# Turning gated activation tiles by a transposing DMA on 16-bit halves instead of on TensorE

## The chip, the cores and the metric

The kernel runs on one core of one Trainium2 chip. TensorE multiplies (its operands come from SBUF, its results go to banks in PSUM), VectorE and ScalarE work element by element, SP issues DMAs, and each engine runs its own list of instructions in order, waiting on semaphores. The metric is the device time of one execution in microseconds; lower is better.

## The reference

One layer on a sequence of 256 tokens of width 2048, in 32-bit floating point: a half-step SwiGLU feed-forward block (FFN 1), a token-mixing layer (a recurrent branch and a gated convolution behind one input projection and ahead of one output projection), and a second feed-forward block (FFN 2). The change lies in the feed-forward blocks, whose inner width is 5632:

```
def swiglu_ffn(x, w_gate, w_up, w_down):
    return (jax.nn.silu(x @ w_gate) * (x @ w_up)) @ w_down
...
x = x + FFN_RESIDUAL_SCALE * swiglu_ffn(rms_norm(x, ffn1_norm[l]),
                                        ffn1_w_gate[l], ffn1_w_up[l], ffn1_w_down[l])
```

## The kernel before

**Products.** Every 32-bit product is made of three products in `F32R`. A weight unit is 512 rows by 512 columns (128 partitions x 4 x 512, 1 MB); SP loads it into `raw`, ScalarE casts it in two halves of 128x1024 into `hi`, VectorE subtracts to get `lo` (128x2048). The stationary operand, the activations, has a high and a low of its own, and `multiply` runs high x hi, low x hi and high x lo: 12 matmuls of 128x512 for one half of the tokens (t = 0 or 1), 24 for both. Buffers for `raw` (three, and two longer kept ones) and for `hi`/`lo` (two, and one more) limit how far ahead the other engines can work.

**Groups.** The inner width is 11 units of 512. Unit 0 comes first, alone (`begin` in FFN 1, `begin_after` in FFN 2). The others come in five pairs, s = 0 to 4, units 1 + 2s and 2 + 2s. For each pair `seven` makes the gate group and then the up group, each with seven products in place of eight for half of the contraction (a Strassen-like scheme with sums of blocks, `raw <- raw - raw` on VectorE) and plain products for the rest. `gate` and `up` are called as results are done: `up` multiplies into the tile `sg[t, n]` (128 tokens x 512 columns; in the profile these tiles are named `u_g`, `z` and `s_g`, and `sg` for unit 0), first for n = 1, then for n = 0.

**Turning.** For the product with the down weights a tile must have its columns on the partitions. `turn_hidden(u, t, h, again)` makes four TensorE transposes of 128x128 into the PSUM bank `ph`, ScalarE casts the result to the high part of `hidden[u]`, VectorE subtracts for the low part, and where `again` is set (even s) ScalarE copies the turned tile back, for the sums of blocks. The calls are put into `waiting` and made by `settle` a little later, so that TensorE has other matmuls meanwhile.

**Down.** After s = 0, 2 and 4 `down` multiplies the units that are ready: after s = 0 units 0, 1, 2; after s = 2 units 3 to 6; after s = 4 units 7 to 10. The output has four columns of 512: column 0 by `product`, then sums of blocks of the last two units m and n, then columns 1 and 2 by `seven`, then column 3 by `product`. In `product` the order of units is the older ones, n, m.

**Order.** The kernel is written in a framework that schedules: it puts the instructions of each engine in an order of its own, by its estimates, except where the kernel pins program order. So the order on an engine is not that of the code.

Of the kernel before, what the change touches and what calls it, by code (L numbers as in the profile page):

```python
# [9 lines left out]

F32 = mybir.dt.float32
F32R = mybir.dt.float32r
AF = mybir.ActivationFunctionType
ALU = mybir.AluOpType
AX = mybir.AxisListType

P = 128
# [3 lines left out]
NT = S // P  # L21
KD = D // P
KF = FF // P
CW = 512
NC_D = D // CW
UK = 4
# [22 lines left out]
def hybrid_block(ctx: ExitStack, tc: tile.TileContext, a: dict, out: bass.AP):  # L49
# [32 lines left out]
    def bank(name):  # L82
        return psum.tile([P, 512], F32, tag="ps", name=name)
# [128 lines left out]
    class Norm:  # L212
# [5 lines left out]
        def squares(self, c, engines=(act, act)):  # L218
            for t, engine in enumerate(engines):
                x, part = xres[:, t, c * CW : (c + 1) * CW], self.ss[:, t, c : c + 1]  # L220
                if engine is dve:
                    junk = work.tile([P, CW], F32, tag="junkv", name=f"junkv_{self.name}_{c}_{t}", bufs=1)
                    dve.scalar_tensor_tensor(junk, x, 1.0, x, op0=ALU.mult, op1=ALU.mult, accum_out=part)
# [69 lines left out]

    def product(w, c, us, y, name, stagger=False, between=None):
        ps = [bank(f"ps_{name}_{t}") for t in range(NT)]
        cs = slice(c * CW, (c + 1) * CW)
        late = []
        for i, u in enumerate(us):  # L300
            blk = unit(w[u * UK * P : (u + 1) * UK * P, cs], f"{name}_{u}")
            begin, end = i == 0, i == len(us) - 1
            if stagger and i >= len(us) - 2:
                late.append((u, blk, begin, end))
            else:
                multiply([(ps[t], stationary(y(u), t), begin, end) for t in range(NT)], blk)
            if between:
                between(i)
            pump(1.5)
        for t in range(NT):  # L310
            for u, blk, begin, end in late:
                multiply([(ps[t], stationary(y(u), t), begin, end)], blk)
        return ps

# [101 lines left out]
    def ffn(tag, norm, after, opening=False):  # L416
        with (
# [7 lines left out]
            def keep(name, dt=F32):  # L425
                return fp.tile([P, CW], dt, tag="keep", name=name, bufs=13)

            hidden = {}
            turned = {}
            waiting = []  # L430
# [17 lines left out]
            def settle():  # L448
                while waiting:
                    turn_hidden(*waiting.pop(0))  # L450


            units, vs, sf, ready = [], {}, {}, []

# [41 lines left out]
            def begin():  # L496
# [26 lines left out]
                for j in range(UK):  # L523
                    for t in range(NT):
# [1 line left out]
                        pe.matmul(gps[t], yh, blk[j][0], start=j == 0, stop=False)  # L526
                        pe.matmul(gps[t], yl, blk[j][0], start=False, stop=False)
                        pe.matmul(gps[t], yh, blk[j][1], start=False, stop=j == UK - 1)
                norm.squares(0, (dve, dve))
                for c in (1, 2):  # L530
                    norm.squares(c, (dve, act))

                def tokens(u):
                    n = [keep(f"n{tag}_{u}_{t}") for t in range(NT)]
# [36 lines left out]
                norm.squares(3, (dve, act))  # L571
# [49 lines left out]
                for t in range(NT):  # L621
                    sg = keep(f"sg{tag}_0_{t}")
                    act.activation(sg, gps[t], AF.Silu)
                    dve.tensor_tensor(sg, ups[t], sg, op=ALU.mult)
                    waiting.append((0, t, sg, False))

            def begin_after():
                follow = {
                    (0, "g"): [flush],
                    (0, "u"): [norm.factor, lambda: plain(0)],  # L630
                    (1, "g"): [norm.rows, lambda: plain(1), lambda: normalise(0)],
                    (1, "u"): [lambda: normalise(1), sums, lambda: plain(2)],
                    (2, "g"): [lambda: normalise(2), lambda: plain(3)],
                }
                for u in range(KD // UK):
                    for m in "gu":
                        blk = parts_of(first_columns(m, u), f"{m}{tag}_0_{u}")
                        multiply([(ps[m, t], stationary(norm.xT[u], t), u == 0, u == 3) for t in range(NT)], blk)
                        pump(1.5)
                        for fn in follow.get((u, m), ()):  # L640
                            fn()
                units.append(big(f"x{tag}_3"))
                for t in range(NT):
                    sg = keep(f"sg{tag}_0_{t}")
                    act.activation(sg, ps["g", t], AF.Silu, scale=norm.r[:, t : t + 1])
                    dve.scalar_tensor_tensor(
                        sg, ps["u", t], norm.r[:, t : t + 1], sg, op0=ALU.mult, op1=ALU.mult
                    )
                    waiting.append((0, t, sg, False))

            (begin if opening else begin_after)()
            xs = list(enumerate(units))[2:]
            turn_of["hold"] = False

            def down(last):
                us = sorted(set(hidden) | {w[0] for w in waiting})
                m, n = us[-2:]
# [8 lines left out]
                for c in (0, 3):  # L666
                    end = last and tag == 2 and c == NC_D - 1
                    ps = product(
                        wd, c, us[:-2] + [n, m], hidden.get, f"d{tag}_{m}_{c}", end,
                        (lambda i: settle()) if c == 0 else None,  # L670
                    )
                    Engine.pinned = end
                    for t in range(NT):
                        update(c, t, ps[t])
                    if c == 0:
                        sh = {}
                        seven_of(
                            sh, hidden[m], hidden[n],
                            {(t, i): turned[u, t] for t in range(NT) for i, u in ((0, m), (1, n))},
                            quad(keep(f"hspare{tag}_{m}")),  # L680
                            [[quad(keep(f"hs{tag}_{m}_{i}_{z}", F32R)) for z in range(2)] for i in range(4)],
                        )()
                        got = {}

                        def add(t, b, ps, tiles):
                            got[t, b] = [ps] + tiles
                            if (0, b) in got and (1, b) in got:
                                for i in range(NT):
                                    update(2 - b, i, *got[i, b])

                        if tag == 1 and m == 5:
                            prepare()
                        seven(wd, (m, n), (2 * CW, CW), sh, [(u, hidden[u]) for u in us[:-2]], f"d{tag}_{m}", keep, add)
                hidden.clear()
                turned.clear()

            for s in range(5):
# [15 lines left out]

                def up(t, n, ps, tiles):
                    dve.tensor_tensor(sg[t, n], total(ps, tiles), sg[t, n], op=ALU.mult)
                    if (t, n) == (1, 0):
                        settle()
                    waiting.append((1 + 2 * s + n, t, sg[t, n], s % 2 == 0))

                def meanwhile(i):  # L720
                    if i == 1:
                        settle()
                    elif s == 0 and not opening:
# [347 lines left out]
```

## Time and profile before

| | |
|---|---|
| median of 3 runs | 1739.5 us (1739.38 to 1740.49) |
| profiled execution, its own time | 1741.48 us |
| span of the profiled execution | 1739.7 us |
| TensorE clock granted | 0.999 |
| busy: TensorE, VectorE, ScalarE | 1721.9, 1485.2, 1042.1 us |
| DMA, mean share of 16 engines on SP's queue | 57.2% |
| `ph`: busy on TensorE, ScalarE, VectorE | 22.97, 37.06, 28.16 us |

Busy is the time in which an engine has an instruction running; on TensorE one matmul overlaps the next, so sums of durations are more than the time that passes. In the rows, `out<-in` are the program's names with buffer numbers left out, `x` is a count, and a bracket or a last column names the idle time ahead of an instruction and what ended it.

### The profile page before, as it was taken

The numbers are of one execution on the slowest core, as the hardware profiler recorded it, in microseconds if no ns is written. First come the engines' busy times: TensorE is split into PE (matmuls) and PEld (weight loads), VectorE is DVE, ScalarE is ACT, GpSimd is POOL, SyncE is SP. The second block draws the span as 40 slices with busy tenths as digits, with TensorE's granted clock in tenths as the row PEclk, the third lists the DMA queues.
The fourth block names the chain that finished last, engine by engine and source line by source line (L and its number), as shares of the span: only waits on it lengthen the run. The fifth ranks groups of instructions, "written<-read, shape, count | busy, mean of one in ns | idle before, by whom it ended". The sixth has DMA issues, their size and how long they took to land. (4 is left out here: it accounts for less than half of the span.)

```text
span 1739.7 us, 20328 instructions
## 1 busy us (share of the span) xinstructions
PE 1721.9 (99%) x8035; PEld 1436.1 (83%) x8035; DVE 1485.2 (85%) x1233; ACT 1042.1 (60%) x1345; POOL 6.9 (0%) x32
## 2 busy tenths in 40 slices
PE   8999999999999999999999999999999999999997
PEld 6888888888888888888888888888788888888886
DVE  7998999889789898687986668989799888899895
ACT  6765566656466656565655555656556664656654
POOL 1000000000000000000000000000000000000000
PEclk9999999999999999999999999999999999999999
DMA  8564665575466656555556663575475546555742
GB/s 299 191 213 145 218 214 197 182 254 205 159 209 203 199 188 216 172 170 194 177 189 209 224 203 129 199 243 185 160 252 201 206 144 231 193 194 194 255 174 104
DMA packets 173920, 343.24 MB, mean 197 GB/s; under 512 B 5636, under 2 KB 8064, under 8 KB 173696
## 3 DMA queue, kind: packets, MB, share of 16 engines
q1 hardware_dynamic: 173360, 340.82, 57.2%
q8 instruction: 63, 1.03, 0.2%
q10 hardware_dynamic: 144, 1.05, 0.1%
q14 instruction: 33, 0.27, 0.0%
q0 software_dynamic: 320, 0.07, 0.0%
HBM read 339.82 MB, written 2.10 MB: 197 GB/s over the span
## 5 line engine op out<-in xcount | busy, mean ns | idle before, releaser
L42 ACT CAST hi_g_p<-raw_g 128x1024 fp32r<-128x1024 f32 x132 | 134.3, 1049 | 97.8 <-DVE raw_g L42 27.6
L42 ACT CAST hi_u_p<-raw_u 128x1024 fp32r<-128x1024 f32 x140 | 140.8, 1047 | 73.1 <-DVE raw_u L42 26.8
L42 DVE TENSOR_TENSOR lo_g_p<-raw_g,hi_g_p 128x2048 fp32r<-128x2048 f32 x66 | 150.2, 2285 | 30.2 <-ACT hi_g_p L42 29.9
L42 DVE TENSOR_TENSOR lo_u_p<-raw_u,hi_u_p 128x2048 fp32r<-128x2048 f32 x70 | 159.0, 2286 | 19.3 <-ACT hi_u_p L42 18.9
L42 PE MATMUL ps_d<-hi_d,h 128*128 128x512 f32 x704 | 168.0, 390 | 0.0
L42 PEld LDWEIGHTS ps_d<-hi_d,h 128*128 128x128 f32 x704 | 131.5, 188 | 27.0
L42 PE MATMUL ps_in<-xT_nm,hi_in 128*128 128x512 f32 x640 | 153.3, 391 | 0.0
L42 PEld LDWEIGHTS ps_in<-xT_nm,hi_in 128*128 128x128 f32 x640 | 117.4, 188 | 23.3 <-ACT tha L42 0.3
L42 ACT CAST hi_d<-raw_d 128x1024 fp32r<-128x1024 f32 x88 | 88.2, 1047 | 68.2 <-PE ps_u_d L42 22.4
L42 DVE TENSOR_TENSOR lo_d<-raw_d,hi_d 128x2048 fp32r<-128x2048 f32 x44 | 100.6, 2290 | 31.0 <-ACT hi_d L42 31.0
L42 DVE TENSOR_TENSOR lo_in<-raw_in,hi_in 128x2048 fp32r<-128x2048 f32 x40 | 91.3, 2286 | 38.8 <-ACT hi_in L42 38.2
L42 ACT CAST hi_in<-raw_in 128x1024 fp32r<-128x1024 f32 x80 | 80.0, 1045 | 67.1 <-PE ps_in L42 45.8
L42 ACT CAST hi_d_p<-raw_d 128x1024 fp32r<-128x1024 f32 x84 | 84.3, 1047 | 50.2 <-DVE raw_d L42 39.4
L42 ACT CAST hi_g_x<-raw_g 128x1024 fp32r<-128x1024 f32 x80 | 81.3, 1048 | 47.5 <-PE ps_g_c L42 25.3
L42 DVE TENSOR_TENSOR lo_d_p<-raw_d,hi_d_p 128x2048 fp32r<-128x2048 f32 x42 | 95.4, 2286 | 11.8 <-ACT hi_d_p L42 11.7
L42 ACT CAST hi_u_x<-raw_u 128x1024 fp32r<-128x1024 f32 x80 | 80.5, 1047 | 33.9 <-PE ps_u_c L42 21.8
L42 DVE TENSOR_TENSOR raw_u<-raw_u,raw_u 128x2048 f32<-128x2048 f32 x40 | 91.6, 2290 | 9.0 <-DMA raw_u<-in_ffn_w_up_dram 8.3
L42 DVE TENSOR_TENSOR lo_g_x<-raw_g,hi_g_x 128x2048 fp32r<-128x2048 f32 x40 | 91.3, 2284 | 5.5 <-ACT hi_g_x L42 5.3
L42 DVE TENSOR_TENSOR raw_g<-raw_g,raw_g 128x2048 f32<-128x2048 f32 x37 | 84.5, 2286 | 9.3 <-DMA raw_g<-in_ffn_w_gate_dram 8.9
L42 DVE TENSOR_TENSOR lo_u_x<-raw_u,hi_u_x 128x2048 fp32r<-128x2048 f32 x40 | 91.4, 2284 | 0.8 <-ACT hi_u_x L42 0.5
L42 PE MATMUL ps_d<-lo_d,h 128*128 128x512 f32 x352 | 87.3, 389 | 0.0
L42 PEld LDWEIGHTS ps_in<-xT_nm,lo_in 128*128 128x128 f32 x640 | 82.1, 191 | 3.1
(391 smaller groups left out, 3592.2 us busy)
## 6 DMA issues: line engine op xcount, KB each, us to landing
raw_d<-in_ffn_w_down_dram SPq DMA_DIRECT2D x88, 1024.0 KB, 5.1
raw_u<-in_ffn_w_up_dram SPq DMA_DIRECT2D x87, 1024.0 KB, 5.2
raw_g<-in_ffn_w_gate_dram SPq DMA_DIRECT2D x86, 1024.0 KB, 5.2
raw_in<-in_w_in_dram SPq DMA_DIRECT2D x40, 1024.0 KB, 5.0
raw_o<-in_w_out_dram SPq DMA_DIRECT2D x16, 1024.0 KB, 5.1
xres<-in_x_dram SPq DMA_DIRECT2D x4, 512.0 KB, 7.6
raw_u<-in_ffn_w_up_dram SPq DMA_DIRECT2D x2, 512.0 KB, 9.3
raw_g_first<-in_ffn_w_gate_dram SPq DMA_DIRECT2D x1, 1024.0 KB, 11.9
```

The costliest lines, as they stand in the source:

```text
L42: ins = getattr(self.engine, name)(*args, **kwargs)
```

## The change

`turn_hidden` is now called at once instead of through `waiting`. ScalarE copies the tile, read as 16-bit numbers, into `plane` with all first halves ahead of all second halves; one DMA on SP's queue transposes the eight 128x128 blocks of 16-bit numbers from `plane` back into the tile; ScalarE copies it into `plane` again so that the halves join to 32-bit numbers; from there the high, the low and the second copy are made as before. There is one buffer for `plane`. The squares that VectorE makes use it as scratch too, instead of one of their own. `down` holds the banks of columns 0 and 3 at the same time and goes through them by a plan: the older units and n for column 0, the older units for column 3 (with one older unit also n), then m for column 0, the sums of blocks, and the rest of column 3 ahead of `seven`, or behind it in the last one.

```
-                pt = bank(f"ph{tag}_{u}_{t}")
-                for j in range(UK):
-                    pe.transpose(pt[:, j * P : (j + 1) * P], h[:, j * P : (j + 1) * P], ident)
+                pt = plane()
+                mixed = "p (f b) -> p b f"
+                flat = "p (b f) -> p b f"
+                act.copy(pt.bitcast(U16).rearrange(flat, b=2), h.bitcast(U16).rearrange(mixed, b=2))
+                nc.sync.dma_start(
+                    h.bitcast(U16).rearrange("p (r c) -> p r c", c=P), pt.bitcast(U16), transpose=True
+                )
+                act.copy(pt.bitcast(U16).rearrange(mixed, b=2), h.bitcast(U16).rearrange(flat, b=2))
                 pt = pt.rearrange("p (j c) -> p j c", j=UK)
...
-                norm.squares(0, (dve, dve))
+                norm.squares(0, (dve, dve), plane)
...
-                    waiting.append((0, t, sg, False))
+                    turn_hidden(0, t, sg, False)
...
+                def add_units(c, units):
+                    blks = [
+                        (u, unit(wd[u * UK * P : (u + 1) * UK * P, c * CW : (c + 1) * CW], f"d{tag}_{m}_{c}_{u}"))
+                        for u in units
+                    ]
...
+                plan = [(0, [u]) for u in others + [n]] + [(3, [u]) for u in others]
+                if len(others) == 1:
+                    plan.append((3, [n]))
+                plan.append((0, [m]))
+                tail = [(3, [n, m])] if end else [(3, [u]) for u in (n, m) if (3, [u]) not in plan]
+                for step in plan:
+                    add_units(*step)
+                block_sums()
+                if not last:
+                    for step in tail:
+                        add_units(*step)
...
+                seven(wd, (m, n), (2 * CW, CW), sh, [(u, hidden[u]) for u in others], f"d{tag}_{m}", keep, add)
+                if last:
+                    for step in tail:
+                        add_units(*step)
...
-                    if (t, n) == (1, 0):
-                        settle()
-                    waiting.append((1 + 2 * s + n, t, sg[t, n], s % 2 == 0))
+                    turn_hidden(1 + 2 * s + n, t, sg[t, n], s % 2 == 0)
```

Three places in the order, all in FFN 1; the places in FFN 2 read alike.

TensorE, end of the up group of s = 2 and start of its down (m = 5, n = 6), before:

```order
L42 MATMUL ph_6_1_2710<-ident,u_g_2_2332 128x128 x4
L42 MATMUL ph_6_0_2718<-ident,u_g_2_2283 128x128 x4
L42 MATMUL ps_u_2_d<-hi_u_2_p_2726,x_1_201 128x512 x8
L42 MATMUL ps_u_2_d<-lo_u_2_p_2727,x_1_201 128x512 x4
L42 MATMUL ps_d_5_0_0_2745<-hi_d_5_0_3_2749,h_3_2250 128x512 x8
L42 MATMUL ps_d_5_0_1_2746<-hi_d_5_0_3_2749,h_3_2250 128x512 x8
L42 MATMUL ps_d_5_0_0_2745<-lo_d_5_0_3_2750,h_3_2250 128x512 x4
L42 MATMUL ps_d_5_0_1_2746<-lo_d_5_0_3_2750,h_3_2250 128x512 x4
L42 MATMUL ph_5_1_2779<-ident,z_2_2432 128x128 x4
L42 MATMUL ph_5_0_2787<-ident,s_g_2_2199 128x128 x4
```

The same place now, where `ps_d_5_0` is column 0 and `ps_d_5_3` column 3 of the down of units 3 to 6 (`h_3` to `h_6`), the first matmuls of each step:

```order
L43 MATMUL ps_u_2_d<-hi_u_2_p_2722,x_1_201 128x512 x8
...
L43 MATMUL ps_d_5_0_0_2748<-hi_d_5_0_3_2754,h_3_2135 128x512 x8
...
L43 MATMUL ps_d_5_0_0_2748<-hi_d_5_0_4_2785,h_4_2026 128x512 x8
...
L43 MATMUL ps_d_5_0_0_2748<-hi_d_5_0_6_2816,h_6_2603 128x512 x8
...
L43 MATMUL ps_d_5_3_0_2750<-hi_d_5_3_3_2847,h_3_2135 128x512 x8
...
L43 MATMUL ps_d_5_3_0_2750<-hi_d_5_3_4_2878,h_4_2026 128x512 x8
...
L43 MATMUL ps_d_5_0_0_2748<-hi_d_5_0_5_2909,h_5_2714 128x512 x8
```

The transposes are gone, and m (`h_5`) is first used in the sixth unit instead of the fourth.

ScalarE, end of the up group of s = 1 and start of the gate group of s = 2, before:

```order
L42 CAST hi_u_1_p_2143<-raw_u_1_10_1888 128x1024 x2
L42 CAST hi_g_2_p_2182<-raw_g_2_00_2166 128x1024 x2
L42 CAST hi_g_2_p_2202<-raw_g_2_00_2166 128x1024
L42 CAST h_4_2128<-ph_4_1_2129 128x4x128
L42 CAST h_4_2128<-ph_4_0_2136 128x4x128
L42 CAST hi_g_2_p_2202<-raw_g_2_00_2166 128x1024
```

The same place now; `plane<-u_g` of 128x1024 is the parting copy, of 128x2x512 the joining one:

```order
L43 COPY plane_2027<-u_g_1_1745 128x1024
L43 CAST hi_u_1_p_2142<-raw_u_1_10_1882 128x1024 x2
L43 CAST hi_g_2_p_2187<-raw_g_2_00_2171 128x1024
L43 COPY plane_2027<-u_g_1_1745 128x2x512
L43 CAST hi_g_2_p_2187<-raw_g_2_00_2171 128x1024
L43 CAST h_4_2026<-plane_2027 128x4x128
L43 COPY plane_2052<-u_g_1_1696 128x1024
L43 CAST hi_g_2_x_2226<-raw_g_2_21_2175 128x1024
L43 CAST hi_g_2_p_2207<-raw_g_2_00_2171 128x1024
L43 COPY plane_2052<-u_g_1_1696 128x2x512
L43 CAST hi_g_2_p_2207<-raw_g_2_00_2171 128x1024
L43 CAST h_4_2026<-plane_2052 128x4x128
```

Three casts stand between the parting and the joining copy of the first tile, two between those of the second, and half casts of the weights stand behind each joining copy.

SP at the down of s = 2, now (before, the same loads without the transposing DMAs):

```order
L168 DMA raw_d_5_0_6_2814<-in_ffn_w_down_dram 128x4x512
L431 DMA_TRANSPOSE u_g_2_2322<-plane_2604 128x8x128
L168 DMA raw_d_5_3_3_2845<-in_ffn_w_down_dram 128x4x512
L168 DMA raw_d_5_3_4_2876<-in_ffn_w_down_dram 128x4x512
L168 DMA raw_d_5_0_5_2907<-in_ffn_w_down_dram 128x4x512
L431 DMA_TRANSPOSE u_g_2_2273<-plane_2630 128x8x128
L168 DMA raw_d_5_3_6_2961<-in_ffn_w_down_dram 128x4x512
L168 DMA raw_d_5_3_5_2992<-in_ffn_w_down_dram 128x4x512
L431 DMA_TRANSPOSE z_2_2422<-plane_2715 128x8x128
```

A transposing DMA stands behind and ahead of weight loads, and waits there for its parting copy.

More of the change, by code (lines that the diff above doesn't have):

```diff
@@ L221, in squares @@
                 if engine is dve:
-                    junk = work.tile([P, CW], F32, tag="junkv", name=f"junkv_{self.name}_{c}_{t}", bufs=1)
-                    dve.scalar_tensor_tensor(junk, x, 1.0, x, op0=ALU.mult, op1=ALU.mult, accum_out=part)
+                    dve.scalar_tensor_tensor(spare(), x, 1.0, x, op0=ALU.mult, op1=ALU.mult, accum_out=part)
                 else:
@@ L292, in columns, with product @@
         return ps
-    def product(w, c, us, y, name, stagger=False, between=None):
+    def product(w, c, us, y, name):
         ps = [bank(f"ps_{name}_{t}") for t in range(NT)]
         cs = slice(c * CW, (c + 1) * CW)
-        late = []
         for i, u in enumerate(us):
             blk = unit(w[u * UK * P : (u + 1) * UK * P, cs], f"{name}_{u}")
[L302 to L308, printed above, removed]
+            multiply([(ps[t], stationary(y(u), t), i == 0, i == len(us) - 1) for t in range(NT)], blk)
             pump(1.5)
-        for t in range(NT):
-            for u, blk, begin, end in late:
-                multiply([(ps[t], stationary(y(u), t), begin, end)], blk)
         return ps
@@ L426, in keep, with plane @@
                 return fp.tile([P, CW], dt, tag="keep", name=name, bufs=13)
+            def plane():
+                return fp.tile([P, CW], F32, tag="plane", name=f"plane{tag}", bufs=1)
             hidden = {}
             turned = {}
-            waiting = []
             def turn_hidden(u, t, h, again):
@@ L528, in begin @@
                         pe.matmul(gps[t], yh, blk[j][1], start=False, stop=j == UK - 1)
-                norm.squares(0, (dve, dve))
+                norm.squares(0, (dve, dve), plane)
                 for c in (1, 2):
-                    norm.squares(c, (dve, act))
+                    norm.squares(c, (dve, act), plane)
                 def tokens(u):
@@ L570, in begin @@
                 act.copy(hi[:, :2], ru[:, :2])
-                norm.squares(3, (dve, act))
+                norm.squares(3, (dve, act), plane)
                 norm.factor()
@@ L648, in begin_after @@
                     )
-                    waiting.append((0, t, sg, False))
+                    turn_hidden(0, t, sg, False)
             (begin if opening else begin_after)()
@@ L655, in down @@
             def down(last):
-                us = sorted(set(hidden) | {w[0] for w in waiting})
-                m, n = us[-2:]
+                us = sorted(hidden)
+                others, (m, n) = us[:-2], us[-2:]
+                end = last and tag == 2
                 def update(c, t, *parts):
@@ L664, in update @@
                         after(c, t)
[L666 to L693, printed above, removed]
@@ new lines, in down @@
+                side = {c: [bank(f"ps_d{tag}_{m}_{c}_{t}") for t in range(NT)] for c in (0, 3)}
+                def add_units(c, units):
[3 more added lines that the diff above has]
+                    ]
+                    groups = [[0], [1]] if end and units == [n, m] else [[0, 1]]
+                    for ts in groups:
+                        for u, blk in blks:
+                            multiply(
+                                [(side[c][t], stationary(hidden[u], t), u == us[0], u == m) for t in ts], blk
+                            )
+                            pump(1.5 / len(groups))
+                    if units[-1] == m:
+                        Engine.pinned = end and c == 3
+                        for t in range(NT):
+                            update(c, t, side[c][t])
@@ new lines, in down, with block_sums, add @@
+                sh, got = {}, {}
+                def block_sums():
+                    seven_of(
+                        sh, hidden[m], hidden[n],
+                        {(t, i): turned[u, t] for t in range(NT) for i, u in ((0, m), (1, n))},
+                        quad(keep(f"hspare{tag}_{m}")),
+                        [[quad(keep(f"hs{tag}_{m}_{i}_{z}", F32R)) for z in range(2)] for i in range(4)],
+                    )()
+                def add(t, b, ps, tiles):
+                    got[t, b] = [ps] + tiles
+                    if (0, b) in got and (1, b) in got:
+                        for i in range(NT):
+                            update(2 - b, i, *got[i, b])
@@ L694, in down @@
+                if tag == 1 and m == 5:
+                    prepare()
+                seven(wd, (m, n), (2 * CW, CW), sh, [(u, hidden[u]) for u in others], f"d{tag}_{m}", keep, add)
+                if last:
+                    for step in tail:
+                        add_units(*step)
                 hidden.clear()
```

10 lines of the change are left out of this document (3 added, 7 removed).

## The prediction

> **What bounds the kernel now.** I read the page first, then who TensorE waited for, then the tile of the transposes, then the timelines of the places where they stand.
>
> ```profile
> span 1739.7 us, 20328 instructions
> PE 1721.9 (99%) x8035; PEld 1436.1 (83%) x8035; DVE 1485.2 (85%) x1233; ACT 1042.1 (60%) x1345; POOL 6.9 (0%) x32
> PE pt_n L42 <- DMA xres<-in_x_dram: 3.4, 1, 3.4
> PE pv_first L42 <- POOL ident masks.py:199: 2.4, 1, 2.4
> PE ps_d_a L42 <- DVE lo_d_p L42: 1.1, 2, 0.9
> ```
>
> TensorE is busy for 99% of the span, and the list of its waits is short: two at the start, then one of 1.1 us in total. So a matmul taken away shortens the kernel by its own pace, and a wait put in front of TensorE lengthens it by all of the wait, because TensorE has no idle time in which to catch up. VectorE (85%) is the next engine, ScalarE has 40% free. The profiled execution took 1741.5 us, its span 1739.7; the median of the three runs is 2.0 us below the profiled time. I sum against 1741.5 and take 2 off at the end.
>
> **What leaves TensorE.** In the view of the tile `ph` the transposes are 80 + 40 + 40 + 16 = 176 matmuls; the timeline shows eight per pair of tiles.
>
> ```profile
> L42 PE MATMUL ph<-ident,u_g x80: 270/272/273, 137.7 to 1642.0; 128*128 128x128 f32 x80
> L42 PE MATMUL ph<-ident,z x40: 272/272/273, 146.8 to 1650.6; 128*128 128x128 f32 x40
> L42 PE MATMUL ph<-ident,s_g x40: 272/273/273, 147.2 to 1651.1; 128*128 128x128 f32 x40
> L42 PE MATMUL ph<-ident,sg x16: 270/272/275, 65.1 to 1089.5; 128*128 128x128 f32 x16
> 1390.11 1.03 PE L42 MATMUL ph<-ident,u_g 128*128 128x128 f32 x8
> 1390.90 2.07 PE L42 MATMUL ps_u_d<-hi_u_p,x 128*128 128x512 f32 x8
> 1393.72 3.79 PE L42 MATMUL ps_d<-hi_d,h 128*128 128x512 f32 x16
> 1405.50 3.79 PE L42 MATMUL ps_d<-hi_d,h 128*128 128x512 f32 x16
> 1410.94 3.79 PE L42 MATMUL ps_d<-hi_d,h 128*128 128x512 f32 x16
> L42 ACT CAST h<-ph x44: 574/588/596, 69.4 to 1651.4; 128x512 fp32r<-128x512 f32 x44
> L42 DVE TENSOR_TENSOR h<-ph,h x44: 673/681/685, 71.6 to 1653.5; 128x512 fp32r<-128x512 f32 x44
> ```
>
> Eight of them take from 1390.11 to 1390.90, 0.79 us; 22 such groups are 22 x 0.79 = **17.4 us**. That is all that can be won: 1741.5 - 17.4 = 1724.1.
>
> **What comes in.** There are 44 turns (the x44 above). Each adds two ScalarE copies of 128x1024 16-bit elements, one that parts the halves and one that joins them, and one DMA of 256 KB on SP's queue. The copies I price by the casts of the same element count:
>
> ```profile
> L42 ACT CAST hi_u_p<-raw_u 128x1024 fp32r<-128x1024 f32 x140 | 140.8, 1047 | 73.1 <-DVE raw_u L42 26.8
> raw_u<-in_ffn_w_up_dram SPq DMA_DIRECT2D x87, 1024.0 KB, 5.2
> raw_g_first<-in_ffn_w_gate_dram SPq DMA_DIRECT2D x1, 1024.0 KB, 11.9
> out_dram<-xres SPq DMA_DIRECT2D x4, 256.0 KB, 2.7
> raw_g<-in_ffn_w_gate_dram SPq DMA_DIRECT2D x2, 256.0 KB, 5.2
> ```
>
> 88 x 1.05 = 92 us more ScalarE, 1134 us in all (65%): affordable on average. What matters is the landing time D of the transposing DMA, which this trace does not show. ScalarE runs in order, and its joining copy stands only two to five instructions behind the parting copy (the order's rows), so beyond those the whole engine waits for the landing, and the casts behind it, the lows that VectorE makes of them, and TensorE with it. From below, D is 2.7 us: 256 KB stored when nothing else is queued. From above, 11.9 us, the slowest landing of a full unit behind others. I take **D = 5.2 us**, nearest to two rows: 256 KB loads that shared the queue took 5.2, and the unit loads that the transposes will stand among take 5.2. This term only adds, so no gain hides in it.
>
> [...] No row here shows a transposing DMA; TensorE's transposes here pass every 0.10 us.
>
> **Odd pairs (4 places).** After the up groups with odd s the turns stand in the start of the next gate group. The first row below is a stretch of 13.5 us with the busy time of TensorE, its loads, VectorE, ScalarE; the others are the timeline there.
>
> ```profile
> 1310.50:1324.00 13.50, 13.50 (x65) 11.25 (x65) 13.50 (x11) 9.60 (x12) 0.00 (x0) 1.00 0.34 109
> 1300.55 2.00 ACT L42 CAST hi_g_p<-raw_g 128x1024 fp32r<-128x1024 f32 x2 [1.63 <-PE ps_u_a L42]
> 1294.82 0.68 DVE L42 TENSOR_TENSOR u_g<-u_u,u_g 128x512 f32<-128x512 f32 x1
> 1302.58 2.29 DVE L42 TENSOR_TENSOR lo_g_p<-raw_g,hi_g_p 128x2048 fp32r<-128x2048 f32 x1 [1.33 <-ACT hi_g_p L42]
> 1311.71 2.28 DVE L42 TENSOR_TENSOR lo_g_p<-raw_g,hi_g_p 128x2048 fp32r<-128x2048 f32 x1
> 1321.12 2.28 DVE L42 TENSOR_TENSOR lo_g_p<-raw_g,hi_g_p 128x2048 fp32r<-128x2048 f32 x1
> 1314.85 1.07 PE L42 MATMUL ps_g_c<-lo_g_p,xs 128*128 128x512 f32 x4
> 1323.91 1.07 PE L42 MATMUL ps_g_a<-lo_g_p,xs 128*128 128x512 f32 x4
> ```
>
> VectorE is full in this stretch (13.50 of 13.50), and the two lows that end at 1313.99 and 1323.40 are used at 1314.85 and 1323.91: margins of 0.86 and 0.51 us, the smallest of the pair. With D = 5.2: turn 1 starts at 1295.5, lands at 1301.8, and its join pushes the second half of the first `hi_g_p` by 1.2 us, which VectorE absorbs in part. Turn 2 can part when the one `plane` has been read, at 1306.7 (the cast ends at 1303.8, its low at 1306.1, the low of h takes 0.6); it has parted at 1307.75, lands at 1307.75 + 5.2 = 1312.95, joins to 1314.0, and the second half of the next cast ends at 1315.0, its low (2.29) at 1317.3. TensorE wants it at 1314.85 - 0.79 = 1314.06: **3.2 us late**. Turn 3 finds `plane` read at 1318.0 (low of h behind that late low), has parted by 1319.1, lands at 1324.3, join 1325.35, two casts and the high of h (1.05 + 0.59 + 1.05) to 1328.0, low to 1330.3; wanted at 1323.91 - 1.58 + 3.2 = 1325.5: **4.8 us late**. Turn 4 has five instructions (4.8 us) of cover: 0.4, within the slack. 8.0 us per place, x 4 = **32 us**. With D = 2.7 the same walk gives 1.1 + 2.3 = 3.4, x 4 = 14.
>
> **Even pairs (6 places).** Here down follows, and the interleaving moves the use of the last tiles back.
>
> ```profile
> 1379.56 1.28 DVE L42 TENSOR_TENSOR u_g<-u_u,u_g 128x512 f32<-128x512 f32 x2
> 1380.32 2.00 ACT L42 CAST hi_u_p<-raw_u 128x1024 fp32r<-128x1024 f32 x2 [1.11 <-PE ps_u_a L42]
> 1393.90:1416.50 22.60, 22.60 (x105) 18.79 (x105) 20.38 (x19) 14.10 (x20) 0.00 (x0) 1.00 0.41 140
> ```
>
> The four turns share one `plane`, so they go one after another: parting, D, joining, high and second copy (0.59 each), with five casts of 1.05 between by the order. From the first parting at 1381.4 (behind the first `hi_u_p` cast) the last low is ready at 1381.4 + 4 x 3.28 - 0.59 + 5 x 1.05 + 0.68 + 4D = 1399.9 + 4D. A down unit takes 1410.94 - 1405.50 = 5.44 us on TensorE, and the first starts at 1393.72 - 0.79 = 1392.9. With two older units (s = 2, 4) unit m comes after five steps, at 1420.1: covered up to D = 5.05, so 0.6 us at 5.2. With one older unit (s = 0) it comes after four, at 1414.7, and the order has a sixth cast but an earlier start (1399.7 + 4D): covered up to 3.75, so 5.8 us late. I use the same stretch for both. Per FFN 5.8 + 0.6 + 0.6 = 7.0, twice = **14 us**. Each further microsecond of D costs four here, in every place: the steepest term.
>
> **Opening pairs (4 turns).** The order covers them with about 3.7, 4.2, 1.7 and 3.7 us (casts of 1.05, copies of 0.59). 1.5 + 1.0 + 3.5 + 1.5 = 7.5 us of wait in a gate group's start, less 0.86 of margin each: **4 us**.
>
> **At nothing.** Squares into `plane` instead of their own scratch: same instruction. Highs and lows of h read SBUF instead of PSUM: same element counts, 0.59 and 0.68. The tail of column 3 moved ahead of the down group for s = 0 and 2 covers the block sums with 10.9 us; where it stays behind (s = 4) the block sums stay as exposed as now, about the 1.1 us of the first fence. The end of the kernel keeps its order.
>
> **SP.** The transposing DMA waits at SP for the parting copy, and weight loads stand behind it.
>
> ```profile
> SPq L167 <- DVE lo_d L42: 138.1, 38, 7.6
> DVE raw_g L42 <- DMA raw_g<-in_ffn_w_gate_dram: 8.9, 5, 5.4
> ```
>
> SP waits for VectorE to free a buffer before nearly every load (here 138.1 us in 38 waits), so a parting copy that is done within such a wait holds nobody. I price it at nothing, and the opposite below.
>
> **Sum.** 32 + 14 + 4 - 17.4 = +33 us: 1741.5 + 33 - 2 = **1772 us**, slower. Below D of about 3 the same sum turns to a gain.
>
> **Rivals.**
> 1. *The transposes land like a plain 256 KB store* (2.7 us) and ScalarE's free 40% takes the rest. For it: even pairs and openings are then covered, only the two tight lows are left. Against it: the queue is shared with 1 MB loads. Time: between 1741.5 - 17.4 and that plus 14, 1724 to 1738, middle 1731: **faster**. It decides below D = 3. Chance 0.20.
> 2. *The transposing DMA is slow*, because it moves in small blocks: D from 8 us to the 11.9 row. Odd pairs gain two excesses, even ones four each, the openings one per turn. At 8: 4 x 13.6 + 2 x (17.0 + 11.8 + 11.8) + 15 - 17 = +133, 1873 after the 2; at 10: 70 + 129 + 23 - 17 = +205, 1945; at 11.9: +274, 2013. For it: nothing here turns 16-bit halves by DMA. Against it: 3/4 less data than a load. Chance 0.18, taken at 1945.
> 3. *Weight loads come late.* Each of the 16 odd turns holds SP by the 3.2 us by which a parting copy lags, unabsorbed: 16 x 3.2 = 51 on top, 1823. Against it: the waits above. Chance 0.10.
> 4. That the change does not do what it says is excluded: no `ph` stands in TensorE's order any more.
>
> Chances: forecast 0.52, rivals 0.20, 0.18, 0.10. Three measured runs spread by 0.06%; I take 0.2% (3.5 us) as what can be told from no change. Faster by more: most of rival 1, 0.18. Within: 0.05. Slower: 0.77. The range goes down to 1724 (nothing can be below) and up to 1880, which takes in rival 3 and rival 2's lower end; 0.15 lies above.
>
> **What would show it.** Right: TensorE waits of 3 to 5 us for `lo_g_p` after odd pairs, ScalarE waiting on a DMA before the joining copy 44 times, landing times near 5 us, `ph` gone. Wrong: landings of 3 us (rival 1), or 8 and more with waits on `h` at the last column 0 unit in every down (rival 2), or VectorE and ScalarE waiting on weight DMAs far above the 8.9 us of the `raw_g` row above (rival 3).

## The result and the profile after

The changed kernel takes 1769.54 us (median of 4 runs, 1764.18 to 1770.39) against 1739.74 us before (1739.38 to 1740.49, 4 runs): ratio 1.0164, 95% interval 1.0144 to 1.0185. It is slower by 29.8 us; the forecast was 1772. The profiled execution has a span of 1767.5 us.

First the page: the span, and busy time of each engine.

```profile
span 1767.5 us, 20182 instructions
PE 1721.6 (97%) x7859; PEld 1419.8 (80%) x7859; DVE 1486.8 (84%) x1233; ACT 1137.2 (64%) x1433; POOL 6.9 (0%) x32
```

TensorE has 176 instructions less, ScalarE 95 us more work (forecast: 92). But TensorE's busy time is as before, 1721.6 against 1721.9: its matmuls took as much longer as the transposes had taken (in e11 below the same matmuls keep it busy for 1704.0 us).

Whom TensorE waited for (total us, times, longest), with the longest waits in the timeline:

```profile
PE ps_g_c L43 <- ACT hi_g_p L43: 12.0, 3, 6.2
PE ps_d L43 <- DVE h L43: 3.8, 4, 1.9
PE ps_d L43 <- ACT h L43: 3.8, 4, 1.4
PE ps_g_c L43 <- ACT s_g L43: 2.7, 4, 0.7
```

```profile
209.22 1.21 PE L43 MATMUL ps_g_a<-lo_g_p,x 128*128 128x512 f32 x4 [0.26 <-DVE lo_g_p L43]
215.95 3.78 PE L43 MATMUL ps_g_c<-hi_g_p,xs 128*128 128x512 f32 x8 [5.52 <-ACT hi_g_p L43]
219.53 1.91 PE L43 MATMUL ps_g_c<-lo_g_p,xs 128*128 128x512 f32 x4
...
1250.45 2.08 PE L43 MATMUL ps_g_c<-hi_g_p,xs 128*128 128x512 f32 x4 [6.16 <-ACT hi_g_p L43]
...
1695.63 0.50 PE L43 MATMUL ps_d<-hi_d,h 128*128 128x512 f32 x1 [1.32 <-ACT h L43]
1698.04 2.50 PE L43 MATMUL ps_d<-hi_d,h 128*128 128x512 f32 x5 [1.91 <-DVE h L43]
```

The two waits of 5.52 and 6.16 us stand at a place that the prediction does not name: the start of the gate group of s = 1, right behind the first down of each FFN. VectorE is the one that is late there:

```profile
195.00:205.00 10.00, 10.00 (x46) 8.29 (x45) 10.00 (x8) 5.72 (x7) 0.00 (x0) 1.00 0.83 299
```

```profile
209.68 0.69 DVE L43 SCALAR_TENSOR_TENSOR xres<-ps_d_a,xres 128x512 f32<-128x512 f32 x1
210.28 2.28 DVE L43 TENSOR_TENSOR lo_g_x<-raw_g,hi_g_x 128x2048 fp32r<-128x2048 f32 x1
212.48 4.61 DVE L43 TENSOR_TENSOR raw_g<-raw_g,raw_g 128x2048 f32<-128x2048 f32 x2
```

The first fence is a window from 195 to 205 (columns: length, busy time of TensorE, its loads, VectorE, ScalarE, GpSimd, the granted TensorE clock, DMA share, GB/s): VectorE is busy for all of its 10 us. In its timeline it still adds results of down to `xres` at 209.68, and comes to the difference of blocks that ScalarE casts to `hi_g_p` only at 212.48, after TensorE has run dry. Between the two it makes `lo_g_x`, which TensorE uses only later; that order is the framework's, and the point on the tail of column 3 below comes back to it.

In the earlier timeline, the four `lo` matmuls at 219.53 take 1.91 us; at 209.22 they took 1.21. More windows, with the clock in the third column from the end, show why:

```profile
211.90:222.10 10.20, 6.15 (x15) 4.65 (x16) 9.65 (x5) 2.62 (x4) 0.00 (x0) 0.50 0.33 103
222.10:232.10 10.00, 10.00 (x46) 8.27 (x45) 7.16 (x4) 8.13 (x9) 0.00 (x0) 1.00 0.23 67
1246.10:1256.30 10.20, 5.85 (x14) 4.50 (x15) 9.43 (x5) 2.31 (x3) 0.00 (x0) 0.50 0.31 104
1696.70:1703.50 6.80, 5.46 (x13) 4.30 (x14) 6.80 (x6) 2.51 (x3) 0.00 (x0) 0.50 0.01 2
```

From within the two long waits, and from within the second of the pair of 1.32 and 1.91, the clock is at half for 10.2, 10.2 and 6.8 us: 15 matmuls in the first window, 46 in as long a one behind it. From the matmul that ends the last wait to the end of the window are 6.2, 5.8 and 5.5 us; half of these, about 9 us in all, is my estimate of what the slow clock itself cost.

The transposing DMAs and their copies (the view of the tile: nanoseconds min/median/max; then the landing times of all 44; in the second fence, what ScalarE waited for ahead of a copy of this tile):

```profile
L43 ACT COPY plane<-u_g x40: 1037/1196/1372, 126.9 to 1672.5; 128x1024 uint16<-128x1024 uint16 x40
L431 SPq DMA_TRANSPOSE u_g<-plane x20: 1237/1238/2277, 127.9 to 1664.6; - x20
DMA to landing us min/median/max: 3.0/3.6/7.8
```

```profile
ACT plane L43 <- DMA u_g<-plane: 20.6, 14, 4.2
ACT plane L43 <- DVE h L43: 15.1, 9, 2.4
ACT plane L43 <- DMA z<-plane: 12.9, 9, 1.8
ACT plane L43 <- DMA s_g<-plane: 11.0, 8, 3.1
```

A landing takes 3.6 us in the middle, not 5.2. ScalarE waits 44.5 us in 31 waits for landings, and 15.1 us for VectorE to have read the one `plane`.

### The profile page after: what moved, and what is told of

The parts are those of the page before. It is cut to its first block, busy times and chain, and to the rows that moved or that the text cites. A ratio compares the mean times of both kernels' runs of the same rounds, so it can differ in the third digit from the quotient of the medians.

```text
span 1767.5 us, 20182 instructions
## 1 busy us (share of the span) xinstructions
PE 1721.6 (97%) x7859; PEld 1419.8 (80%) x7859; DVE 1486.8 (84%) x1233; ACT 1137.2 (64%) x1433; POOL 6.9 (0%) x32
## 2 busy tenths in 40 slices
DMA packets 220384, 354.76 MB, mean 201 GB/s; under 512 B 52100, under 2 KB 54528, under 8 KB 220160
## 3 DMA queue, kind: packets, MB, share of 16 engines
q10 hardware_dynamic: 144, 1.05, 0.1%
## 5 line engine op out<-in xcount | busy, mean ns | idle before, releaser
L43 PE MATMUL ps_d<-hi_d,h 128*128 128x512 f32 x704 | 172.5, 396 | 7.9 <-DVE h L43 3.8
L43 ACT CAST hi_u_x<-raw_u 128x1024 fp32r<-128x1024 f32 x80 | 80.4, 1047 | 43.9 <-DMA raw_u<-in_ffn_w_up_dram 17.3
```

The lines of the kernel that those rows point to most:

```text
L43: ins = getattr(self.engine, name)(*args, **kwargs)
```

## Experiments

**Theories.** For the first four runs: A, read from the trace after: the new order of down makes the two 6 us waits, the landing costs little. B, the prediction's: the order is free, the landing makes the loss. Edits are to the changed kernel unless another is named; each is compared with runs of the kernel before that were taken beside it (medians 1740.35 us for e1 to e4, 1739.83 for e5 to e8, 1739.89 for e9 to e11, 1739.94 for e12). The framework orders the instructions anew in every kernel, so each edit comes with an order of its own.

**e1: the order alone.** The kernel before with the new `down`; the turns stay on TensorE.

```
                 for step in plan:
                     add_units(*step)
+                    settle()
```

> The kernel before with only the new order of down (columns 0 and 3 interleaved, column 3 done ahead of the down group for s = 0 and 2); the turns stay on TensorE, settled behind the first step. Theory A (from the trace after: the two waits of about 6 us at the gate group behind the first down of each FFN, and the two stretches of half clock behind them, come from the order, because the plain units that let VectorE and ScalarE run ahead are now in front of the down group): slower by 2 x 6 + 2 x 5 = 22 us, 1755 to 1765 us, with the same two waits on ps_g_c. Theory B (as in the prediction: the order costs nothing, all of the loss is the DMA's landing): 1738 to 1742 us, no such waits.

1744.46 us, ratio 1.0025 (1.0015 to 1.0034): +4.1 us. Its timeline at the same place:

```profile
208.36 1.20 PE L42 MATMUL ps_g_c<-hi_g_p,xs 128*128 128x512 f32 x4 [0.63 <-ACT hi_g_p L42]
214.79 2.11 PE L42 MATMUL ps_g_c<-hi_g_x,x 128*128 128x512 f32 x8 [0.68 <-ACT s_g L42]
219.03 1.20 PE L42 MATMUL ps_g_a<-hi_g_p,xs 128*128 128x512 f32 x4 [1.22 <-ACT hi_g_p L42]
```

The waits are at that gate, but 0.6 to 1.2 us long, and the clock stays up (mean 0.998). A is wrong by a factor of five: the order only opens the place. B is wrong too, by 4.

**e2: the turning alone.** DMA turns with the old `down` (column 0 with m last, the down group, column 3).

```
-                plan = [(0, [u]) for u in others + [n]] + [(3, [u]) for u in others]
...
+                for c in (0, 3):
+                    end = last and tag == 2 and c == NC_D - 1
+                    ps = product(
+                        wd, c, us[:-2] + [n, m], hidden.get, f"d{tag}_{m}_{c}", end,
+                    )
```

> The turns by DMA with the order of down as it was before (column 0 with m last, the down group, then column 3). Theory A: no 6 us waits at the gate groups, but unit m now comes after only two (s = 0) or three plain units of 5.44 us; with the measured landing of 3.6 us the last low is ready at 1399.9 + 14.4 = 1414.3 on the prediction's clock, wanted at 1409.2 (s = 2, 4) and 1403.8 (s = 0): waits of 5.1, 5.1 and 10.3 per FFN, 41 in all, 5 at the odd pairs, 17.4 saved: about 1768 us, up to 1795 if the clock halves behind each. Theory B (landing as priced, 5.2 us): waits of 11.5, 11.5 and 16.7 per FFN, 32 at the odd pairs: 1739.7 + 79 + 32 - 17 = 1834 us.

1785.27 us, ratio 1.0261 (1.0244 to 1.0277): +44.9, within A's 1768 to 1795 and far below B's 1834. TensorE's waits have moved into down:

```profile
PE ps_d L43 <- ACT h L43: 24.7, 9, 4.3
PE ps_d L43 <- DVE h L43: 4.3, 5, 1.9
```

With the turns on the DMA, the new order is worth 15.7 us (1785.27 to 1769.54), though by itself it costs 4.1. The price of the order can't be read without the turning.

**e3: column 3 behind the down group.**

```
-                if not last:
-                    for step in tail:
-                        add_units(*step)
...
-                if last:
-                    for step in tail:
-                        add_units(*step)
+                for step in tail:
+                    add_units(*step)
```

> The changed kernel with one thing undone: for s = 0 and 2 the rest of column 3 stands behind the down group again (as for s = 4). Theory A: the 6 us waits at the gate groups behind the first down and the half clock behind them go, 22 us less: about 1748 us. Theory B (the tail ahead of the down group is what hides the block sums; the waits of the gate group come from the landing of the transposes): the waits at the gate stay, and at four places up to 10.9 us of block sums are uncovered: 1770 to 1810 us.

1757.56 us (1754.81 to 1762.71), ratio 1.0104 (1.0081 to 1.0127): 12 us better than the change, half of A's 22, and against B, which had it no faster. The wait at the gate shrinks and is still there (in FFN 2):

```profile
PE ps_g_c L43 <- ACT hi_g_p L43: 3.7, 2, 3.5
```

**e4: no transposing DMA.** Both copies stay; the turning is left out.

```
-                nc.sync.dma_start(
-                    h.bitcast(U16).rearrange("p (r c) -> p r c", c=P), pt.bitcast(U16), transpose=True
-                )
-                act.copy(pt.bitcast(U16).rearrange(mixed, b=2), h.bitcast(U16).rearrange(flat, b=2))
+                act.copy(pt.bitcast(U16).rearrange(mixed, b=2), h.bitcast(U16).rearrange(mixed, b=2))
```

> The changed kernel without the 44 transposing DMAs: both ScalarE copies of each turn stay, but nothing is transposed (this part of the computation is left out). Theory A: only what hangs on the landing goes, about 5 us at the odd pairs, 10 to 14 in the downs and 3.4 of half clock; the two 6 us waits and their half clock stay: 1747 to 1752 us. Theory B (landing is all of the loss): 1769.5 minus some 45, 1722 to 1728 us.

1738.09 us, ratio 0.9986 (0.9977 to 0.9996). Between the two theories: the DMAs make 31.4 us, more than A gave them, the 6 us waits among it (longest wait for `hi_g_p` at the gate's `ps_g_c` now 1.0), yet 10 us more remain than B's 1722 to 1728:

```profile
PE ps_g_c L43 <- ACT hi_g_p L43: 3.9, 6, 1.0
PE ps_g_e L43 <- DVE lo_g_x L43: 3.4, 4, 0.9
```

**From here on** the theories are about those 31.4 us. A now says that they are waiting: ScalarE, in order, for each landing, and those behind it. C: the one `plane` makes the turns serial. E (rival 3 of the prediction): SP is held at each transposing DMA, and the weight loads behind it come late. SP does stand there long:

```profile
SPq L431 <- ACT plane L43: 56.9, 15, 10.9
SPq L431 <- ACT hi_d L43: 46.9, 13, 6.8
```

**e5, e6, e7: two planes, with and without later joining.** e7 has the second plane alone; e5 and e6 (with the old order of down) also write the join one turn later.

```
+                planes[0] += 1
+                if planes[0] % 2:
+                    return fp.tile([P, CW], F32, tag="plane", name=f"plane{tag}", bufs=1)
+                return work.tile([P, CW], F32, tag="junk", name=f"plane{tag}", bufs=1)
...
+                waiting.append(finish)
+                settle(1)
```

> The changed kernel with two planes (the second in the scratch of ScalarE's squares) and the joining copy, the high, the low and the second copy of each turn written one turn later, so that ScalarE has other work between parting and joining. Theory A (31 us of the loss, the difference to the kernel without transposing DMAs, are ScalarE and what stands behind it waiting for the landing): about 1738 us, and ScalarE's waits on a DMA for u_g, z and s_g go from 45 us to under 10. Theory B (the last turn is late because the turns' whole chain is long, and deferring makes it longer): 1765 to 1780 us.

> The same two planes and later joining, with the old order of down. Theory A: 4 us less than the kernel above, since the order alone cost 4.1: about 1734 us, faster than the kernel before. Theory B (unit m, now after two or three plain units, still waits for the last turn): 1755 to 1785 us.

> The changed kernel with two planes and nothing else. Theory A (ScalarE's wait for each landing is what costs): 1760 to 1768 us, little gained. Theory C (the turns are late because they share one plane, as the prediction's even pairs have it): the last turn comes earlier by up to three landings and lows, 1740 to 1750 us.

e5 1760.29 us (ratio 1.0111, 1.0095 to 1.0128), e6 1770.52 (1.0177, 1.0162 to 1.0192), e7 1762.02 (1.0131, 1.0116 to 1.0146). ScalarE in e5:

```profile
ACT plane L43 <- DMA s_g<-plane: 20.1, 10, 5.6
ACT plane L43 <- DMA u_g<-plane: 14.3, 10, 3.0
```

In e5 and e6 the edit did not do what A's test needed: e5's ScalarE still waits 37.1 us for landings, since the framework sets the order on the engine and the join still stood soon behind its DMA. So A's 1738 and 1734 us were missed, e6 within B's range and e5 between the two. In e7 the plane explains 7.5 us, which is A's range (1760 to 1768) and less than C's 20 and more; the table below shows that it moved cost. Later joining adds 1.7 us, within the spread. None of the three settles A against E.

**e8: parting on GpSimd**, in the kernel of e6.

```
-                act.copy(pt.bitcast(U16).rearrange(flat, b=2), h.bitcast(U16).rearrange(mixed, b=2))
+                nc.gpsimd.tensor_copy(pt.bitcast(U16).rearrange(flat, b=2), h.bitcast(U16).rearrange(mixed, b=2))
```

> As the second kernel of this call (two planes, later joining, old order), with the parting copy on GpSimd in place of ScalarE. Theory A (the two copies cost some 11 us as ScalarE work, the rest of the kernel without transposing DMAs): half of the 11 us goes, about 1728 us. Theory D (a GpSimd copy of 1024 strided halves takes several microseconds or slows VectorE): slower than the kernel with both copies on ScalarE, 1740 us or more.

1803.26 us, ratio 1.0364 (1.0349 to 1.0380), against 1770.52 in e6: slower, as theory D has it.

```profile
L447 POOL COPY plane<-u_g x20: 1040/2084/3099, 130.6 to 1687.8; 128x1024 uint16<-128x1024 uint16 x20
```

```profile
PE 1732.1 (96%) x7859; PEld 1428.6 (79%) x7859; DVE 1508.4 (84%) x1233; ACT 1098.8 (61%) x1389; POOL 95.3 (5%) x76
```

The tile's view has the copy at 1.0 to 3.1 us there, and in the page VectorE is busy for 1508.4 us, 23.7 more than in e6 (1484.7). Which of the two costs the time is not shown.

**e9: the transposing DMAs on ScalarE's queue.**

```
-                nc.sync.dma_start(
+                nc.scalar.dma_start(
```

> The changed kernel with the 44 transposing DMAs issued on ScalarE's queue in place of SP's, so that the weight loads never stand behind one that waits for its parting copy (186 us of SP's waits in 44 in the changed kernel). Theory A (ScalarE waiting for the landing is the 31 us): no gain, and 44 issues of about 1.24 us more on ScalarE: 1769 to 1776 us. Theory E (the weight loads held on SP are a good part of the 31 us): 1750 to 1760 us even with those issues.

1784.75 us, ratio 1.0240 (1.0217 to 1.0264). No gain, as A says, but 9 us above A's range, and it doesn't clear E: ScalarE now issues the DMAs itself, 44 times 1.25 us, and stands longer for landings (53.8 us in 30 waits, against 44.5 in 31). The tile's view shows the issues on ScalarE, the view of waits what it then stands for:

```profile
L431 ACTq DMA_TRANSPOSE u_g<-plane x20: 1248/1249/1301, 131.9 to 1682.2; - x20
```

```profile
ACT plane L43 <- DMA u_g<-plane: 35.8, 18, 4.9
```

**e10 and e12: transposing DMAs whose result nobody reads.** They go to a scratch tile; the join puts the parted halves back. e12 has two planes, for which two other scratch tiles of the kernel get one buffer instead of two. In e10 to e12 the second copy is made in place, ahead of the low.

```
+                aside = work.tile([P, CW], F32, tag="junk", name=f"aside{tag}", bufs=1)
                 nc.sync.dma_start(
-                    h.bitcast(U16).rearrange("p (r c) -> p r c", c=P), pt.bitcast(U16), transpose=True
+                    aside.bitcast(U16).rearrange("p (r c) -> p r c", c=P), pt.bitcast(U16), transpose=True
                 )
-                act.copy(pt.bitcast(U16).rearrange(mixed, b=2), h.bitcast(U16).rearrange(flat, b=2))
+                act.copy(h.bitcast(U16).rearrange(mixed, b=2), pt.bitcast(U16).rearrange(flat, b=2))
```

> The changed kernel with the 44 transposing DMAs issued as before, behind their parting copies on SP's queue, but into a scratch tile that nobody reads: the joining copy puts the parted halves back, and nothing is transposed (this part of the computation is left out). SP is held and the DMA engines are busy as in the changed kernel, only nobody waits for a landing. Theory A: all 31 us go, 1738 us as without the DMAs. Theory E: only ScalarE's direct waits go, 1750 to 1765 us.

1757.26 us (1751.74 to 1760.16), ratio 1.0093 (1.0073 to 1.0113), in E's range, but for a reason that the edit leaves in: the next parting copy waits until the DMA has read the only plane.

```profile
ACT plane L43 <- DMA aside<-plane: 37.3, 12, 13.0
```

> As the kernel whose transposing DMAs go to a scratch tile that nobody reads (nothing is transposed: the turning is left out), now with two planes, since there ScalarE still waited 37.3 us in 12 waits for the DMA to have read the one plane, 13.0 us at the longest. The transposing DMAs stay on SP's queue behind their parting copies, so the weight loads stand behind them as in the changed kernel. Theory A (all of the cost of the transposing DMAs is ScalarE waiting for them): 1738 to 1742 us, the time without the DMAs. Theory E (SP held by them and the loads behind it are a part): 1750 to 1758 us, no better than with one plane.

1741.27 us, ratio 1.0009 (0.9999 to 1.0018). No wait on a transposing DMA is left on ScalarE, while SP still stands at them, 165 us in all against 186 in the changed kernel. Its longest rows (the first is the wait for the one scratch tile, which this edit brings in):

```profile
SPq L432 <- DMA aside<-plane: 50.0, 24, 4.8
SPq L432 <- ACT plane L43: 43.8, 15, 11.8
SPq L432 <- ACT s_g L43: 26.1, 5, 6.5
SPq L432 <- ACT hi_d L43: 21.8, 8, 3.9
```

So SP's holding, the issues and the traffic of 44 transposing DMAs cost 3.2 us together (1741.27 - 1738.09), and the other 28.3 (1769.54 - 1741.27) are there only where somebody waits for them, or for the one plane that they read. E falls. The runs of the changed kernel lie 6.2 us apart, so the 28.3 are good to a few us. (The second plane goes into the 3.2 as well, since e4 has one.) How the 28.3 divide between ScalarE standing still and turned tiles that are late for TensorE is not told by these runs: both go in e12. And the order on the engines differs between the two kernels as well, which matters at the gate of s = 1, below.

**e11: no copies either.** Highs and lows from the unturned tile.

```
-                pt = plane()
...
+                pt = h
```

> The changed kernel without the transposing DMAs and without the 88 parting and joining copies: highs and lows are made from the unturned tile (the turning is left out). What both theories use: before 1740.3, less 17.4 of TensorE, plus 4.1 of the order alone = 1727 us, so the copies cost 1738.1 - 1727 = 11 us. Rival: ScalarE's free 40% hides the copies, as the prediction had it, and this kernel takes 1738 us as well; then the 17.4 are not all saved.

1727.17 us, ratio 0.9924 (0.9909 to 0.9938): the 1727 expected. The copies cost 1738.09 - 1727.17 = 10.9 us.

## Right or wrong, point by point

The loss comes out in five steps, each a difference of two runs:

| step | us |
|---|---|
| 176 transposes leave TensorE (e11 less e1; forecast -17.4) | -17.3 |
| the new order of down (e1 less before) | +4.1 |
| 88 copies on ScalarE (e4 less e11) | +10.9 |
| transposing DMAs, not waited for (e12 less e4) | +3.2 |
| waiting for them and for the one plane (after less e12) | +28.3 |
| sum; after less before | +29.2; +29.8 |

Such a chain of differences must add up, but for the 0.6 us between two medians of the kernel before; the sum is no test of the steps.

Where they stand, as time from a stage's first matmul to the next stage's in the traces, both FFNs together (s in brackets; the stages left out differ by under 2 us; in the changed kernel two matmuls of gate (1) stand ahead of the last four of down (0), and the boundary is put behind these):

| | before | e11 | e4 | e12 | after | e7 |
|---|---|---|---|---|---|---|
| gate (0), openings | 83.5 | 83.7 | 84.1 | 88.3 | 83.5 | 87.7 |
| down (0) | 128.9 | 125.4 | 125.3 | 126.4 | 133.8 | 129.0 |
| gate (1) | 83.9 | 88.4 | 88.8 | 88.7 | 99.7 | 89.4 |
| gate (2), (4): odd pairs | 166.8 | 164.0 | 174.6 | 172.3 | 173.0 | 182.6 |
| down (2) | 171.0 | 169.1 | 169.1 | 169.1 | 172.6 | 169.1 |
| down (4) and the end | 182.8 | 179.2 | 179.3 | 179.1 | 188.3 | 184.9 |
| up groups | 417.7 | 409.4 | 408.4 | 408.5 | 410.0 | 408.4 |

- **The transposes, -17.4: right.** e11 came out where this saving and e1 together put it (17.3 measured).
- **The landing time D, 5.2 us: wrong.** 3.6 measured, nearer to the 256 KB store (2.7) than to the loads it was taken from (5.2); the fastest landing took 3.0 us, the slowest 7.8. **Rival 2**, slow landings: refuted. The transposing DMAs do move in small packets (the changed kernel has 52,100 packets under 512 B, the kernel before 5,636), but no run shows its 8 to 11.9 us as the usual landing: the medians are 3.4 to 4.3 us in the changed kernel and in e2, e5, e8, e9, e10 and e12, and only single landings took as long (8.8 us in e5, 16.2 in e10).
- **Odd pairs, 32 us: the term that failed most.** They cost 173.0 - 164.0 = 9.0 us, and e4, which has no landings, pays 10.6 there. So it is the copies, not the landing. The waits for `lo_g_p` of 3.2 and 4.8 us, the first sign that the prediction named, are not there (0.3 us at the longest). In the changed kernel the second turn's joining copy found its data almost landed, and TensorE's next wait there is 0.67 us for a ScalarE copy:

```profile
1329.59 1.05 ACT L43 COPY plane<-u_g 128x1024 uint16<-128x1024 uint16 x1 [2.44 <-DVE h L43]
1333.79 1.36 ACT L43 COPY plane<-u_g 128x1024 uint16<-128x1024 uint16 x1 [0.25 <-DMA u_g<-plane]
1340.99 2.11 PE L43 MATMUL ps_g_c<-hi_g_x,x 128*128 128x512 f32 x8 [0.67 <-ACT s_g L43]
```

- **Copies "affordable on average": wrong.** 92 us of work on an engine with 40% free cost 10.9 us, and e4 pays nearly all of it (10.6) at the odd pairs, which have 16 of the 44 turns. An average over the span says nothing of a stage.
- **Even pairs, 14 us: right in kind.** The downs cost 8.4 + 3.5 + 9.1 = 21.0 us over e11, with TensorE waiting for `h` (7.6 us in the view of its waits; the rest is not traced to a wait, beyond the half clock). The sizes differ: s = 4, priced at 0.6 per FFN, cost 9.1 in the two, most of it in FFN 2, where the 1.32 and 1.91 us waits shown above stand, with 6.8 us of half clock.
- **"The tail of column 3 moved ahead: nothing": wrong, and the missing term.** The gate of s = 1, behind that tail, costs 15.8 us more than before. About 5 us come with the order of down alone, which leaves no plain units behind the down group for VectorE and ScalarE to run ahead in: e11, which has that order and no turns, takes 88.4 there, against 83.9 before and 81.6 in e2 with the old order. The other 11, part of it at half clock (10.2 us in each FFN of the changed kernel), are, among the kernels with this order, in the changed kernel and e9 alone. In these two VectorE makes `lo_g_x` ahead of the difference of blocks, as the timeline at the start shows; in e1, e4, e5, e7 and e10 to e12 the framework puts the difference first, as here in e4:

```profile
203.32 2.29 DVE L43 TENSOR_TENSOR raw_g<-raw_g,raw_g 128x2048 f32<-128x2048 f32 x1 [0.29 <-DMA raw_g<-in_ffn_w_gate_dram]
206.13 2.28 DVE L43 TENSOR_TENSOR lo_g_x<-raw_g,hi_g_x 128x2048 fp32r<-128x2048 f32 x1
```

  In these seven TensorE waits at most 1.5 us for that difference, and the stage takes 88 to 90 us, also in e5 and e7, where ScalarE waits 37 and 38 us for landings. So the 11 us are not the price of landings as such: VectorE comes late out of the down, and the order that the framework chose makes it later. e3 points the same way: in its FFN 1 the difference stands first and TensorE does not wait for it, in its FFN 2 `lo_g_x` does and TensorE waits 3.5 us. No run has the lateness with the other order, so how the 11 us divide stays open.
- **Openings, 4 us:** nothing.
- **SP at nothing: nearly right** (3.2 us with traffic and issues), so rival 3 is refuted. **Rival 1** had the landing almost right and the outcome wrong: even free landings leave 1738 us.

So the forecast of 1772 was right by luck, by a sum of errors: odd pairs 23 too high, openings 4, against gate (1) with some 16 not priced and the downs 7 too low.

The table also shows what the second plane did in e7: downs and gate (1) get 22 us shorter, 10 of them at gate (1) with its other order; odd pairs and openings get 14 longer. No version here is faster than the kernel before and still turns its tiles.

## What to carry to other kernels

Moving work off the engine that bounds is paid by what must wait on the new path, not by its busy time: here 17.3 us saved met 28.3 us that are gone when nobody waits for the transfers, and 10.9 us of copies on an engine with 40% free. Plain work between two dense stages is slack for the engines behind the bound (gate (1) took 83.9 us before, and 88.4 in e11 without such work ahead of it); price an order together with the latency that it has to cover, since the same order cost 4.1 us without it and gained 15.7 with it. Where a framework orders the instructions, compare the orders on the engines before a difference of two kernels is put down to the edit: here some 11 us stand at a place where it chose another one. To tell a transfer's own cost from the cost of awaiting it, keep the transfer and let nobody read it, and make sure that nobody waits for its source either.

## What the runs showed of the hardware

- The granted clock fell to 0.50 about 1.5 and 1.8 us into waits of 5.5 and 6.2 us, and about 0.6 us into one of 1.9 that came soon behind one of 1.3; it stayed there for 10.2, 10.2 and 6.8 us. In e2 the mean clock was 0.987, in the changed kernel 0.991, in the kernel before 0.999.
- In the changed kernel a transposing DMA of 256 KB within SBUF landed in 3.0 / 3.6 / 7.8 us (min, median, max) and held its issuing queue for 1.24 us in the middle (1.23 to 2.28), where a 1 MB load just ahead of one took 0.37:

```profile
1317.76 0.37 SPq L168 DMA_DIRECT2D raw_g<-in_ffn_w_gate_dram  x1
1319.44 1.24 SPq L431 DMA_TRANSPOSE u_g<-plane  x1
```

- ScalarE's copy of 128x1024 16-bit numbers took 1.04 to 1.05 us where it parts the halves and 1.34 to 1.37 where it joins them.
